# Two decoder layers on one Trainium2 core: the last MLP's second tile in banks of 512, 256 and 256 columns, and a mean square that ACT adds at the layer boundaries

## The chip, the cores and the metric

The kernel runs on one core of a Trainium2 chip. The metric is the device time of one execution in microseconds (us). Five engines work side by side, each through its own queue in order: PE (TensorE, matrix products; "PEld" is its weight load), DVE (VectorE), ACT (ScalarE), POOL (GpSimd) and SP (SyncE, which here issues DMAs). An engine waits for another by a semaphore; what stands behind a waiting instruction in its queue waits too.

## The reference, cut to what matters

Two layers run over 256 tokens of 1024 features. Each layer has a mixer (block-sparse and indexed attention) and a gated MLP of width 2816, both in the same sandwich:

```
h = rms_norm(x, g_pre) * (1 + scale) + shift
y = token_mixer(h)            # or: (gelu(conv3(h @ w_up_act)) * (h @ w_up_lin)) @ w_down
x = x + gate * rms_norm(y, g_post)

rms_norm(v, g) = v * rsqrt(mean(v * v) + 1e-6) * g      # mean over the 1024 features, per token
```

So each of the four sub-layers ends with the mean square of `y` per token, and three of them go on with the mean square of the new `x`, before the next product can start. The last sub-layer ends with the output's DMA.

## The kernel before, in words

The 256 tokens are two tiles of 128 rows (t = 0 and 1). Weights come through a stream of 1 MB DMAs into `raw` and are split there into a high and a low fp32r part: ACT copies the high one (`wh`, `dh`, line 139), DVE subtracts it for the low one (`wl`, `dl`, line 140). Every product is then three passes on PE (`mm3`, lines 567 to 569, or `project`, line 391): high x high, low x high, high x low.

The MLP goes through 22 blocks of 128 hidden features. `up(i)` makes a block's hidden activations, 24 matmuls of 256 columns for each of the two branches, and `down` multiplies them by `w_down`: for each tile t two PSUM banks of 512 output columns, `ys[t]`, three matmuls for each bank and block. The banks collect all 22 blocks. 17 of the blocks go through `down` between the `up`s; the last five follow at the end, first tile 0's two banks, then tile 1's.

`residual` ends a sub-layer for one tile. For each bank it takes the squares' sum over 512 columns on ACT (`square`, line 254, an activation and a read of its accumulator) and multiplies by the gate on DVE (line 318). `inv_root` then lets POOL add the two sums and EPS (line 262) and raise that to -0.5 (line 264), and DVE adds the result to `xt` (line 326). At the very end the pieces are sent to DRAM from there, tile 1 in pieces of 512, 256 and 256 columns.

`boundary` joins two sub-layers. There are three: mixer to MLP in layer 0 (near 153 to 175 us in the trace), MLP to the next layer's mixer (near 342 to 366 us), and mixer to MLP in layer 1 (near 483 to 506 us). In each, `stat` takes the mean square of the new `xt` in two halves on ACT and `inv_root` again finishes it on POOL; `norm_T` scales by it on DVE (line 286) and PE turns the result (line 274); `mod_T` makes `hh` and `hl` from it, on ACT (lines 297, 307, 305) and DVE (lines 300, 309). PE's next products need these.

The order on each engine is not the order of the code. A scheduler places the instructions by its own estimates, except where the code pins them or says that one is issued after another; so an added or lengthened instruction can move others.

Of the kernel before, what the change touches and what calls it, by code (L numbers as in the profile page):

```python
# [12 lines left out]
BF = mybir.dt.bfloat16  # L13
AF = mybir.ActivationFunctionType
OP = mybir.AluOpType
AX = mybir.AxisListType

D = 1024
S = 256
DEPTH = 2  # L20
HD = 64
FF = 2816
NF = FF // 128
EPS = 1e-6
# [50 lines left out]
def trunk(ctx: ExitStack, tc, plan, x, c, stream, small, rope, out):  # L75
    nc = tc.nc
# [10 lines left out]
    def bank(i):  # L87
        return ps.tile([128, 512], F32, name=f"b{i}", tag=f"b{i}")
# [7 lines left out]
    def t2(dt=F32):  # L96
        return wrk.tile([128, 512], dt, name="t2", tag="t2", bufs=12)
# [4 lines left out]
    def tiny(n):  # L102
        return wrk.tile([128, n], F32, name=f"tiny{n}", tag=f"tiny{n}", bufs=8)
# [113 lines left out]
    def pre_scale(l, which):  # L217
        a = wrk.tile([128, 8], F32, name="prescale", tag="prescale", bufs=2)
        o = 8 if which == "mix" else 32
        nc.vector.scalar_tensor_tensor(out=a, in0=mods[l][:, o:o + 8], scalar=1.0,  # L220
                                       in1=scol(l, "g_pre_" + which)[:, :8], op0=OP.add, op1=OP.mult)
        return a, mods[l][:, o - 8:o]
# [29 lines left out]
    def square(src, n, s, to=None):  # L252

        nc.scalar.activation(out=t2(BF) if to is None else to, in_=src, func=AF.Square, scale=float(n) ** -0.5, accum_out=s)  # L254

    def inv_root(s):

        r = tiny(1)
        if s.shape[-1] == 1:
            nc.gpsimd.tensor_scalar(out=r, in0=s, scalar1=EPS, scalar2=None, op0=OP.add)  # L260
        else:
            nc.gpsimd.tensor_scalar(out=r, in0=s[:, 0:1], scalar1=s[:, 1:2], scalar2=EPS, op0=OP.add, op1=OP.add)
        r2 = tiny(1)
        nc.gpsimd.tensor_tensor(out=r2, in0=r, in1=mhalf, op=OP.pow)
        return r2
# [11 lines left out]
    def stat(t):  # L277
        s = tiny(2)
        for h in range(2):
            square(xt[:, t, 512 * h:512 * h + 512], D, s[:, h:h + 1])  # L280
        return inv_root(s)

    def norm_T(t, r, banks):
        xn = [t2(), t2()]
# [26 lines left out]

    def residual(t, y, g, to=None):

        s = tiny(2)
        d = [t2(), t2()]
        for h in range(2):
            square(y[h], D, s[:, h:h + 1])
            nc.vector.tensor_tensor(out=d[h], in0=y[h], in1=g[:, 512 * h:512 * h + 512], op=OP.mult)
            if h == 0:
                yield  # L320
        r = inv_root(s)
        yield
        parts = [(0, 512), (512, 256), (768, 256)] if to is not None and t else [(0, 512), (512, 512)]
        for i, (o, n) in enumerate(parts):
            xo = xt[:, t, o:o + n]
            nc.vector.scalar_tensor_tensor(out=xo, in0=d[o // 512][:, o % 512:o % 512 + n], scalar=r, in1=xo,
                                           op0=OP.mult, op1=OP.add)
            if to is not None:
                (nc.scalar if i % 2 else nc.sync).dma_start(to[:, o:o + n], xo)
        yield  # L330

    def boundary(ys, g, scale, bias, hh, hl):

        r0, r1 = residual(0, ys[0], g), residual(1, ys[1], g)
        for _ in range(3):
            next(r0)
        s0 = stat(0)
        next(r1)
        p0 = norm_T(0, s0, (4, 5))
        next(r1)  # L340

        def second(ins):
            with tc.issue_after(ins):
                next(r1)

        a = mod_T(p0, 0, scale, bias, hh, hl, second)
        s1 = stat(1)
        p1 = norm_T(1, s1, (6, 4))
        return a, mod_T(p1, 1, scale, bias, hh, hl)
# [216 lines left out]
    def mm3(y, hh, hl, wh, wl, first, last):  # L566
        nc.tensor.matmul(y, lhsT=hh, rhs=wh, start=first, stop=False)  # L567
        nc.tensor.matmul(y, lhsT=hl, rhs=wh, start=False, stop=False)  # L568
        nc.tensor.matmul(y, lhsT=hh, rhs=wl, start=False, stop=last)  # L569
# [10 lines left out]
    def half(a, h):  # L580
        return a[:, 512 * h:512 * h + 512]
# [181 lines left out]
    for l in range(DEPTH):  # L763
# [90 lines left out]
        ys = [[bank(0), bank(1)], [bank(2), bank(3)]]  # L854
# [40 lines left out]
        scale, bias = pre_scale(l, "ffn")  # L895
# [5 lines left out]
        ys = [[bank(0), bank(1)], [bank(2), bank(3)]]  # L901
# [22 lines left out]
        def up(i):  # L924
# [27 lines left out]
            nc.vector.tensor_tensor(out=al, in0=av, in1=ah.bitcast(F32), op=OP.subtract)  # L952
            pend.append((i, ah, al, dh, dl))

        def down(items, tiles):
            for t in tiles:
                tt = slice(128 * t, 128 * t + 128)
                for h in range(2):
                    for i, ah, al, dh, dl in items:
                        mm3(ys[t][h], ah[:, tt], al[:, tt], half(dh, h), half(dl, h), i == 0, i == NF - 1)  # L960
                        yield

        for i in range(NF):
            if i == 3 + 4 * l:
                bg.add("ada", gemv_v(l, 40, 48, 4))
                bg.add("ada", gate_rows(l, "ffn"))
                if l + 1 < DEPTH:
                    bg.add("ada", gemv_v(l + 1, 0, 32, 5))
            bg.run(up(i))
            if i < NF - 3 and len(pend) > 2:  # L970
                bg.run(down([pend.pop(0)], (0, 1)))
        bg.drain("ada")
        gate = gates["ffn"]
        bg.run(down(pend, (0, 1)))
        tps["free"] = [6, 7]
        if l + 1 < DEPTH:
            hh, hl = hT_tiles()
            scale, bias = pre_scale(l + 1, "mix")

            placed = boundary(ys, gate, scale, bias, hh, hl)  # L980
        else:
            for t in range(2):
                for _ in residual(t, ys[t], gate, out[0, 128 * t:128 * t + 128, :]):
                    pass
# [79 lines left out]
```

## Time and profile before

| | us |
|---|---|
| median of 3 runs (lowest, highest) | 689.65 (689.32, 689.72) |
| the profiled execution | 690.58 |
| its span, first to last instruction | 688.8 |
| busy in the span: PE, DVE, ACT, POOL | 665.0, 549.9, 424.8, 26.2 |

PE is busy for 97% of the span at a mean granted clock of 0.995 of full speed, so the time is PE's work plus the few places where it waits, plus the tail behind its last matmul. The profiled execution's own time is 1.8 us above its span and 0.9 us above the median. Columns of the views used here: start, duration, engine, line, operation, what it writes and reads, shapes, count; in brackets the idle time before and what ended it. A matmul's duration is its whole passage through the array; what a stream of them costs is the distance between starts. Lines are those of the kernel before.

### The profile page before, as it was taken

Reading aid. Unit: us, or ns where it says so; the run is one execution under the profiler, and the core shown is the slowest. Engines: PE = TensorE matmul, PEld = TensorE weight load, DVE = VectorE, ACT = ScalarE, POOL = GpSimd, SP = SyncE. Lnnn points to the kernel's source line nnn. Section 1 sums busy time; section 2 is a strip of 40 time slices with the busy share of each in tenths; the row PEclk is TensorE's granted clock in tenths of the full one; section 3 lists DMA queues with packets and bytes.
Section 4 is the critical chain, followed back from the end, with each engine's and each line's share of the span. In section 5 each row is a group of like instructions: output and inputs, shape, how many; then the busy total and the mean of one; then the engine's idle time right before and its main releaser. Section 6 shows DMA issues by size and latency. Waiting matters only on the chain.

```text
span 688.8 us, 11284 instructions
## 1 busy us (share of the span) xinstructions
PE 665.0 (97%) x4311; PEld 570.4 (83%) x4311; DVE 549.9 (80%) x1088; ACT 424.8 (62%) x786; POOL 26.2 (4%) x56
## 2 busy tenths in 40 slices
PE   7999898999999999999999999999999999999996
PEld 4787676777999999999988677777789999999994
DVE  5898999978899999897679985677689876666553
ACT  5566677886955555455576558868696555555441
POOL 1000000002000000000020000000200000000001
PEclk9999999999999999999999999999999999999999
DMA  9999548963489999987436732346246885644001
GB/s 363 419 415 378 181 169 331 368 248 122 184 319 376 380 365 340 341 326 282 163 151 240 279 131 116 123 166 218 107 164 236 303 332 179 224 184 183 1 1 62
DMA packets 24519, 163.04 MB, mean 237 GB/s; under 512 B 3313, under 2 KB 3729, under 8 KB 6161
## 3 DMA queue, kind: packets, MB, share of 16 engines
q1 hardware_dynamic: 23184, 159.77, 61.6%
q0 software_dynamic: 704, 2.11, 1.1%
q8 instruction: 34, 0.56, 0.3%
q10 hardware_dynamic: 576, 0.43, 0.2%
q14 instruction: 21, 0.16, 0.1%
HBM read 161.24 MB, written 1.06 MB: 236 GB/s over the span
## 4 chain that ended last, share of the span: by engine, by line
PE 76%; DVE 12%; ACT 6%; issue 3%; POOL 1%; DMA 1%; SPq 0%; POOLq 0%; DVEq 0%; ACTq 0%
PE b L569 18%; PE b L567 18%; PE b L568 18%; PE b L391 13%; DVE wl L140 3%; PE b L411 3%; DVE raw L684 2%; DVE iscore L434 2%; ACT t L479 1%; PE b L494 1%; ACT t L254 1%; DMA raw<-in_stream_dram 1%; PE b L726 1%; DVE iscore L446 1%; PE b L274 1%
## 5 line engine op out<-in xcount | busy, mean ns | idle before, releaser
L140 DVE TENSOR_TENSOR wl<-raw,wh 128x1024 fp32r<-128x1024 f32 (+1 forms) x146 | 173.1, 1197 | 36.8 <-ACT wh L139 31.2
L567 PE MATMUL b<-hh,wh 128*128 128x256 f32 x640 | 180.1, 281 | 0.0
L569 PE MATMUL b<-hl,wh 128*128 128x256 f32 x640 | 179.7, 281 | 0.0
L568 PE MATMUL b<-hh,wl 128*128 128x256 f32 x640 | 179.7, 281 | 0.0
L139 ACT ACTIVATE wh<-raw 128x1024 fp32r<-128x1024 f32 (+1 forms) x146 | 148.9, 1046 | 43.9 <-PE b L569 36.2
L568 PEld LDWEIGHTS b<-hh,wl 128*128 128x128 f32 x640 | 122.5, 191 | 1.3
L567 PEld LDWEIGHTS b<-hh,wh 128*128 128x128 f32 x640 | 120.2, 188 | 1.5
L569 PEld LDWEIGHTS b<-hl,wh 128*128 128x128 f32 x640 | 120.2, 188 | 0.0
L189 DVE SCALAR_TENSOR_TENSOR raw<-raw,crow 128x1024 f32<-128x1024 f32 x72 | 86.7, 1220 | 1.3 <-DMA raw<-in_stream_dram 1.3
L391 PE MATMUL b<-wh,hh 128*128 128x512 f32 (+1 forms) x184 | 73.0, 400 | 0.1
L391 PE MATMUL b<-wh,hl 128*128 128x512 f32 (+1 forms) x184 | 68.8, 389 | 0.0
L140 DVE TENSOR_TENSOR dl<-raw,dh 128x1024 fp32r<-128x1024 f32 (+2 forms) x47 | 56.9, 1213 | 13.7 <-ACT dh L139 12.9
L139 ACT ACTIVATE dh<-raw 128x1024 fp32r<-128x1024 f32 (+2 forms) x47 | 49.5, 1058 | 25.9 <-PE b L568 25.9
L944 ACT ACTIVATE t<-b,smt 128x256 f32<-128x256 f32 x44 | 25.0, 569 | 57.9 <-PE b L569 57.9
L567 PE MATMUL b<-dh,t 128*128 128x512 f32 x152 | 59.7, 393 | 0.0
L568 PE MATMUL b<-dh,t 128*128 128x512 f32 x152 | 59.6, 392 | 0.0
L569 PE MATMUL b<-dl,t 128*128 128x512 f32 x152 | 59.2, 389 | 0.0
L391 PE MATMUL b<-wl,hh 128*128 128x512 f32 (+1 forms) x184 | 56.6, 398 | 0.9 <-DVE wl L140 0.9
L391 PEld LDWEIGHTS b<-wh,hh 128*128 128x128 f32 x184 | 34.7, 188 | 8.7 <-issue 1.7
L391 PEld LDWEIGHTS b<-wl,hh 128*128 128x128 f32 x184 | 34.5, 193 | 7.2 <-DVE wl L140 1.2
L391 PEld LDWEIGHTS b<-wh,hl 128*128 128x128 f32 x184 | 34.0, 189 | 6.2 <-issue 0.6
L945 DVE SCALAR_TENSOR_TENSOR t<-b,smt,t 128x255 f32<-128x255 f32 x44 | 21.2, 482 | 20.6 <-ACT t L944 20.4
(172 smaller groups left out, 1100.0 us busy)
## 6 DMA issues: line engine op xcount, KB each, us to landing
raw<-in_stream_dram SPq DMA_DIRECT2D x143, 1024.0 KB, 6.3
raw<-in_stream_dram SPq DMA_DIRECT2D x8, 804.0 KB, 9.9
gate<-gated POOLq DMA_DIRECT2D x4, 512.0 KB, 8.5
xt<-in_x_dram SPq DMA_DIRECT2D x2, 512.0 KB, 4.2
raw<-in_stream_dram SPq DMA_DIRECT2D x1, 984.0 KB, 4.9
out_dram<-xt SPq DMA_DIRECT2D x2, 256.0 KB, 2.1
raw<-in_stream_dram SPq DMA_DIRECT2D x1, 328.0 KB, 5.1
out_dram<-xt ACTq DMA_DIRECT2D x1, 256.0 KB, 2.1
```

The costliest lines, as they stand in the source:

```text
L139: put(nc.scalar.activation(out=hi[:, :n], in_=raw, func=AF.Copy))
L140: put(nc.vector.tensor_tensor(out=lo[:, :n], in0=raw, in1=hi[:, :n].bitcast(F32), op=OP.subtract))
L189: nc.vector.scalar_tensor_tensor(out=ri, in0=ri, scalar=1.0, in1=crow, op0=OP.mult, op1=OP.mult, accum_out=mods[l][:, j + i:j + i + 1])
L391: mm = lambda l_, k, i, start=False, stop=False: nc.tensor.matmul(a[:, :n], lhsT=l_[:, k, tt], rhs=w[k][i], start=start, stop=stop)
L411: ins = nc.tensor.matmul(out, lhsT=lhsT, rhs=rhs, **flags)
L434: nc.vector.scalar_tensor_tensor(out=sc, in0=r[:, j * nk:j * nk + nk], scalar=wi[:, h:h + 1], in1=fill[:, 256 - nk:] if first else sc, op0 ...
L567: nc.tensor.matmul(y, lhsT=hh, rhs=wh, start=first, stop=False)
L568: nc.tensor.matmul(y, lhsT=hl, rhs=wh, start=False, stop=False)
L569: nc.tensor.matmul(y, lhsT=hh, rhs=wl, start=False, stop=last)
L684: pin(nc.vector.scalar_tensor_tensor(out=r, in0=r, scalar=1.0, in1=crow, op0=OP.mult, op1=OP.mult, accum_out=mods[0][:, 8 * a + k:8 * a + ...
L944: nc.scalar.activation(out=z, in_=p[:, :256], func=AF.Identity, scale=w2[:, i:i + 1], bias=bc[:, i:i + 1])
L945: nc.vector.scalar_tensor_tensor(out=z[:, 1:], in0=p[:, :255], scalar=w1[:, i:i + 1], in1=z[:, 1:], op0=OP.mult, op1=OP.add)
```

## The change

Three edits. In the last layer's MLP tile 1's output lies in three banks, one of 512 columns and two of 256 (a part of bank 3, and of bank 7), and `down` runs over these; each 512-column matmul of the former second bank is two of 256. `residual` for this tile takes three sums of squares; POOL adds the first two and EPS, and DVE adds the third when it is there. And in `stat`, at all three boundaries, POOL adds EPS to the first half's sum, and an ACT activation (Identity with a bias) adds the second half's; POOL then has the power alone.

```diff
-    def inv_root(s):
+    def inv_root(s, last=None):
         r = tiny(1)
-        if s.shape[-1] == 1:
-            nc.gpsimd.tensor_scalar(out=r, in0=s, scalar1=EPS, scalar2=None, op0=OP.add)
+        if last is nc.scalar:
+            nc.scalar.activation(out=r, in_=s[:, 1:2], func=AF.Identity, bias=s[:, 0:1])
+        elif last is nc.vector:
+            nc.vector.tensor_tensor(out=r, in0=s[:, 0:1], in1=s[:, 1:2], op=OP.add)
         else:
             nc.gpsimd.tensor_scalar(out=r, in0=s[:, 0:1], scalar1=s[:, 1:2], scalar2=EPS, op0=OP.add, op1=OP.add)
...
             square(xt[:, t, 512 * h:512 * h + 512], D, s[:, h:h + 1])
-        return inv_root(s)
+            if h == 0:
+                nc.gpsimd.tensor_scalar(out=s[:, :1], in0=s[:, :1], scalar1=EPS, scalar2=None, op0=OP.add)
+        return inv_root(s, nc.scalar)
...
+            s, early = tiny(4), tiny(2)
+            for i, (o, n) in enumerate([(0, 512), (512, 256), (768, 256)]):
+                square(y[i], D, early[:, 1:2] if i == 2 else s[:, i:i + 1], t2(BF)[:, :n])
+                if i == 1:
+                    nc.gpsimd.tensor_scalar(out=early[:, :1], in0=s[:, 0:1], scalar1=s[:, 1:2], scalar2=EPS,
+                                            op0=OP.add, op1=OP.add)
+                if i == 2:
+                    r = inv_root(early, nc.vector)
+                nc.vector.tensor_tensor(out=d[o // 512][:, o % 512:o % 512 + n], in0=y[i], in1=g[:, o:o + n],
+                                        op=OP.mult)
...
+        if l == DEPTH - 1:
+            ys[1] = [bank(2), bank(3)[:, :256], bank(7)[:, :256]]
...
-                for h in range(2):
+                o = 0
+                for y in ys[t]:
+                    n = y.shape[-1]
                     for i, ah, al, dh, dl in items:
-                        mm3(ys[t][h], ah[:, tt], al[:, tt], half(dh, h), half(dl, h), i == 0, i == NF - 1)
+                        mm3(y, ah[:, tt], al[:, tt], dh[:, o:o + n], dl[:, o:o + n], i == 0, i == NF - 1)
                         yield
+                    o += n
```

The scheduler also places other work differently with it. The lines of the changed kernel are some 3 to 20 higher for the same instruction (254 stays, 274 is 277, 286 is 291, 297 is 302, 300 is 305, 305 is 310, 307 is 312, 309 is 314, 326 is 345, 391 is 410); line 261 is the new addition on ACT. Numbers behind a name count tiles and differ between the two.

ACT at the boundary from layer 0's MLP to layer 1's mixer, tile 1 (`tiny2` the two sums, `wh` splits of weights that later products need), before:

```order
L254 ACTIVATE t2_3872,tiny2_3869<-xt_69 128x512
L139 ACTIVATE wh_4087<-raw_4085 128x1024
L139 ACTIVATE wh_4091<-raw_4085 128x1024
L297 ACTIVATE hh_3795<-b6_3882,mod1_100,prescale_3797 128x128 x4
L307 ACTIVATE t2_3892<-b6_3882,mod1_100,prescale_3797 128x128 x2
L305 ACTIVATE hh_3795<-t2_3893 128x4x128
L307 ACTIVATE t2_3892<-b6_3882,mod1_100,prescale_3797 128x128 x2
```

and with the change:

```order
L254 ACTIVATE t2_3876,tiny2_3872<-xt_69 128x512
L139 ACTIVATE wh_4091<-raw_4089 128x1024
L261 ACTIVATE tiny1_3878<-tiny2_3872 128x1
L139 ACTIVATE wh_4095<-raw_4089 128x1024
L139 ACTIVATE wh_4101<-raw_4099 128x1024
L302 ACTIVATE hh_3797<-b6_3886,mod1_100,prescale_3799 128x128 x4
L312 ACTIVATE t2_3896<-b6_3886,mod1_100,prescale_3799 128x128 x4
L310 ACTIVATE hh_3797<-t2_3897 128x4x128
```

The addition stands behind a weight split, a third split has come in front of tile 1's `hh`, and `hh`'s second half (line 305, now 310) stands behind four activations of line 307 (now 312) where it stood behind two.

PE at the same place: line 274 (now 277) turns tile 1, `b2` is tile 0's first product in layer 1, `b1` its second, `b0` tile 1's first. Before:

```order
L391 MATMUL b2_3929<-dh_3925,hl_3796 128x328
L274 MATMUL b6_3882<-ident_75,t2_3878 128x128 x4
L274 MATMUL b4_3887<-ident_75,t2_3879 128x128 x4
L391 MATMUL b2_3929<-dh_3925,hl_3796 128x328
L391 MATMUL b1_4015<-wl_4012,hh_3795 128x256
L391 MATMUL b1_4015<-wh_4011,hh_3795 128x256
L391 MATMUL b1_4015<-wl_4012,hh_3795 128x256
L391 MATMUL b0_3967<-dh_3915,hh_3795 128x328
L391 MATMUL b0_3967<-dl_3916,hh_3795 128x328
L391 MATMUL b1_4015<-wh_4011,hh_3795 128x256
```

and with the change:

```order
L410 MATMUL b2_3933<-dh_3929,hl_3798 128x328 x2
L410 MATMUL b1_4019<-wl_4016,hh_3797 128x256
L410 MATMUL b1_4019<-wh_4015,hh_3797 128x256
L410 MATMUL b1_4019<-wl_4016,hh_3797 128x256
L410 MATMUL b1_4019<-wh_4015,hh_3797 128x256
L410 MATMUL b1_4019<-wl_4016,hh_3797 128x256
L410 MATMUL b1_4019<-wh_4015,hh_3797 128x256
L410 MATMUL b1_4019<-wl_4016,hh_3797 128x256
L410 MATMUL b1_4019<-wh_4011,hl_3798 128x256 x4
L410 MATMUL b1_4019<-wh_4015,hl_3798 128x256 x3
L277 MATMUL b6_3886<-ident_75,t2_3882 128x128 x4
L277 MATMUL b4_3891<-ident_75,t2_3883 128x128 x4
```

One matmul of 328 columns and 14 of 256 have come in front of the turn of tile 1, seven more of which (`wl`/`wh` with `hh`, and `hl`) formerly lay between those of `b0`; behind the turn there is now one matmul of `b1`, and then only `b0`: eight on the first half of `hh`, eight on the second, eight on `hl`.

DVE at the third boundary (mixer to MLP, layer 1), tile 0: line 286 (now 291) makes the two halves that PE turns, line 140 is a weight split. Before:

```order
L326 SCALAR_TENSOR_TENSOR xt_69<-t2_5302,tiny1_5311,xt_69 128x512
L318 TENSOR_TENSOR t2_5325<-b2_5035,gate_4127 128x512
L286 TENSOR_SCALAR t2_5330<-xt_69,tiny1_5322 128x512
L140 TENSOR_TENSOR wl_5231<-raw_5224,wh_5230 128x1024
L286 TENSOR_SCALAR t2_5331<-xt_69,tiny1_5322 128x512
```

and with the change:

```order
L345 SCALAR_TENSOR_TENSOR xt_69<-t2_5305,tiny1_5315,xt_69 128x512
L324 TENSOR_TENSOR t2_5329<-b2_5039,gate_4131 128x512
L140 TENSOR_TENSOR wl_5235<-raw_5228,wh_5234 128x1024
L291 TENSOR_SCALAR t2_5335<-xt_69,tiny1_5327 128x512
L291 TENSOR_SCALAR t2_5336<-xt_69,tiny1_5327 128x512
```

Both halves now stand behind the weight split. On ACT the addition for this tile stands behind the split's other half, `wh_5234`. PE's order is the same there as before.

## Rows read from the trace of the kernel before

**Rows 1.** Timeline of PE, last MLP: start, duration, line, operation, shapes, count.
```profile
651.08 0.28 PE L567 MATMUL b<-hh,wh 128*128 128x256 f32 x1
...
668.04 0.40 PE L567 MATMUL b<-dh,t 128*128 128x512 f32 x1
...
678.58 0.40 PE L567 MATMUL b<-dh,t 128*128 128x512 f32 x1
...
681.81 0.40 PE L569 MATMUL b<-wl,t 128*128 128x512 f32 x1
```

**Rows 2.** Timeline of all engines, the tail behind the last matmul.
```profile
682.80 0.19 ACT L254 ACTIVATION_READ_ACCUMULATOR t<-b 128x1 f32 x1
...
683.09 0.30 POOL L262 TENSOR_SCALAR tiny<-tiny 128x1 f32<-128x1 f32 x1 [6.03 <-ACT t L254]
683.47 0.56 POOL L264 TENSOR_TENSOR tiny<-tiny,mhalf 128x1 f32<-128x1 f32 x1
684.07 1.54 DVE L326 SCALAR_TENSOR_TENSOR xt<-t,tiny,xt 128x512 f32<-128x512 f32 x3 [0.35 <-POOL tiny L264]
```

**Rows 3.** ACT by line and form: count, then busy us, mean ns of one.
```profile
L517 ACT ACTIVATE t<-b 128x256 f32<-128x256 f32 x8 | 3.0, 376 | 1.5 <-PE b L411 1.4
...
L517 ACT ACTIVATE t<-b 128x512 f32<-128x512 f32 x4 | 2.3, 582 | 0.0
...
L595 ACT ACTIVATE tiny<-mhalf 128x1 f32<-128x1 f32 x2 | 0.4, 202 | 0.0
```

**Rows 4.** DVE by line and form, one value per row.
```profile
L551 DVE TENSOR_SCALAR tiny<-b 128x1 f32<-128x1 f32 x8 | 1.3, 157 | 4.0 <-PE b L549 4.0
```

**Rows 5.** Timeline of all engines, second boundary (MLP to mixer), tile 1.
```profile
357.54 2.04 ACT L139 ACTIVATE wh<-raw 128x1024 fp32r<-128x1024 f32 x2
357.59 1.21 PE L391 MATMUL b<-dh,hl 128*128 128x328 f32 x7
...
358.77 0.88 DVE L286 TENSOR_SCALAR t<-xt,tiny 128x512 f32<-128x512 f32 x2 [0.94 <-POOL tiny L264]
359.31 1.12 PE L274 MATMUL b<-ident,t 128*128 128x128 f32 x8 [0.51 <-DVE t L286]
...
360.00 1.50 ACT L297 ACTIVATE hh<-b,mod,prescale 128x128 fp32r<-128x128 f32 x4 [0.42 <-PE b L274]
...
361.39 0.82 ACT L307 ACTIVATE t<-b,mod,prescale 128x128 f32<-128x128 f32 x2
...
364.59 1.36 PE L391 MATMUL b<-dh,hl 128*128 128x328 f32 x8
...
365.79 0.28 PE L391 MATMUL b<-wh,hh 128*128 128x256 f32 x1
```

**Rows 6.** Timeline of all engines, third boundary (mixer to MLP, layer 1).
```profile
490.73 1.05 ACT L139 ACTIVATE wh<-raw 128x1024 fp32r<-128x1024 f32 x1
...
491.47 0.48 DVE L286 TENSOR_SCALAR t<-xt,tiny 128x512 f32<-128x512 f32 x1
...
493.77 1.50 ACT L297 ACTIVATE hh<-b,mod,prescale 128x128 fp32r<-128x128 f32 x4
...
496.17 0.66 ACT L305 ACTIVATE hh<-t 128x512 fp32r<-128x512 f32 x1
...
496.89 0.50 PE L391 MATMUL b<-dh,hh 128*128 128x512 f32 x1 [0.50 <-ACT hh L305]
...
500.02 0.55 PE L274 MATMUL b<-ident,t 128*128 128x128 f32 x3 [0.33 <-DVE t L286]
```

**Rows 7.** Timeline of PE, first boundary, turn of tile 1.
```profile
170.29 1.12 PE L274 MATMUL b<-ident,t 128*128 128x128 f32 x8 [0.29 <-DVE t L286]
```

**Rows 8.** Waits of PE over the span: us in total, times, longest.
```profile
PE b L368 <- ACT wh L139: 1.2, 1, 1.2
PE b L368 <- DVE t L362: 1.1, 2, 0.7
```

**Rows 9.** Timeline of DVE, shortly before the first of those waits.
```profile
380.43 2.36 DVE L140 TENSOR_TENSOR wl<-raw,wh 128x1024 fp32r<-128x1024 f32 x2 [0.59 <-PE b L391]
```

More of the change, by code (lines that the diff above doesn't have):

```diff
@@ L312, in residual @@
     def residual(t, y, g, to=None):
-        s = tiny(2)
         d = [t2(), t2()]
-        for h in range(2):
[L317 to L321, printed above, removed]
+        if len(y) == 2:
+            s = tiny(2)
+            for h in range(2):
+                square(y[h], D, s[:, h:h + 1])
+                nc.vector.tensor_tensor(out=d[h], in0=y[h], in1=g[:, 512 * h:512 * h + 512], op=OP.mult)
+                if h == 0:
+                    yield
+            r = inv_root(s)
+        else:
+            s, early = tiny(4), tiny(2)
[8 more added lines that the diff above has]
+                                        op=OP.mult)
+            yield
         yield
@@ L957, in down @@
                 tt = slice(128 * t, 128 * t + 128)
-                for h in range(2):
+                o = 0
+                for y in ys[t]:
+                    n = y.shape[-1]
                     for i, ah, al, dh, dl in items:
-                        mm3(ys[t][h], ah[:, tt], al[:, tt], half(dh, h), half(dl, h), i == 0, i == NF - 1)
+                        mm3(y, ah[:, tt], al[:, tt], dh[:, o:o + n], dl[:, o:o + n], i == 0, i == NF - 1)
                         yield
+                    o += n
         for i in range(NF):
```

## The prediction

> **What bounds the kernel now.** I read the page's busy times first: PE 665.0 us of a span of 688.8, so a term counts only if it lengthens PE's stream, opens or closes a wait of PE, or lies behind its last matmul. Then I read the timelines at the four places that the change touches. In [rows 1] the reader is to see the pitch of the last MLP's stream, from start to start; in [rows 2] the serial chain behind the last square, from ACT's accumulator read over two POOL operations to DVE. [Rows 5 to 7] show the three boundaries, each with a wait of PE for the turned tile, and in [rows 5] how long ACT needs behind the turn before it is done with `hh`. Last I read the waits and what precedes one of them [rows 8, 9], to see whether a shift would be absorbed later.
>
> The sum is made against the profiled execution (span 688.8, own time 690.58, 0.9 above the median) and its difference is put on the median of 689.65. A measurement here can tell about 0.2% from no change, 1.38 us; so "slower" begins at 691.03 and "faster" at 688.27.
>
> **Last MLP, the banks.** 66 matmuls of 512 columns (22 blocks, 3 passes) become 132 of 256. 144 matmuls of 256 lie between 651.08 and 668.04: 16.96/144 = 0.1178 us each. 14 of 512 lie between 678.58 and 681.81: 3.23/14 = 0.2307 [rows 1]. Two of 256 cost 0.2356, so each replaced matmul costs 0.0049 more, and 66 cost **+0.32**. All lie on the stream of a busy PE, so nothing hides them. These 256-column matmuls have a weight load each, as the new ones will, so the pitch is bounded well: zero below, about 0.6 above if the halves cost twice that surplus.
>
> The Trainium skill ("TensorE: Matmul & The Clock Gate", section "Back-to-back issue gap") gives an isolated gap of 262 cycles for 256 columns and 518 for 512; a pair would cost 6 cycles more, 2.5 ns at 2.4 GHz, as an estimate from that page 0.17 us for the 66, and the whole sum would come out at 1.31 us. The trace has 4.9 ns [rows 1], nearly twice that, and the trace decides.
>
> **Last MLP, the tail.** The last square covers 256 columns instead of 512: 376 ns instead of 582 [rows 3], -0.21. Behind its accumulator read (682.80 + 0.19 = 682.99), POOL's addition starts 0.10 later, takes 0.30, and 0.08 later, at 683.47, the power starts: 0.48 [rows 2]. The new chain is ACT to DVE (I take 0.10, as ACT to POOL), one addition of one value (0.157, the nearest DVE row [rows 4]), and DVE to POOL (I take 0.04, the step from the power's end at 684.03 to DVE at 684.07 [rows 2]): 0.30, so -0.18. Handoffs of 0.04 both or 0.10 both give -0.24 and -0.12. Together **-0.39**, and with the banks the last MLP gives -0.07 (0 to -0.13). The third product with the gate on DVE is as long as half of the former one and runs beside the square; it costs nothing.
>
> **The three boundaries, ACT's addition.** By itself the edit replaces POOL's addition between accumulator and power (0.48, as above) by an ACT activation on one value: 0.08 (an engine waiting for its own last result, as POOL does between its two steps), 0.20 ([rows 3], line 595, the nearest form) and 0.10 to POOL, 0.38: -0.10 where it is bound to nothing else. It is an ACT instruction, though, and stands in ACT's queue; what precedes it there is now part of PE's chain.
>
> First boundary. Tile 1's addition follows its accumulator read directly, and PE is idle for 0.29 before the turn [rows 7], so the 0.10 comes through: **-0.10** (0 if the self-wait is 0.18).
>
> The Trainium skill ("ScalarE: Activation LUTs", section "Rules for kernel authors") budgets about 0.3 us for an ACTIVATE whose bias is a pointer operand. The row nearest to ours has 0.20 [rows 3]; no row of before has this form. By the page the gain at this boundary and at tile 1 of the third would be zero, and the sum 0.2 higher.
>
> Second boundary, tile 1 [rows 5]. ACT's addition stands behind one split more than the squares (the order of ACT in the part on the change). Two splits take 2.04 from 357.54, so the first ends at 358.56; then 0.20, 0.10 to POOL and 0.56 for the power: 359.42. DVE has the low split of 1.18 (2.36 for two [rows 9]) in front of both halves of the norm, to 359.8. Before, the norm started at 358.77 and PE turned 0.54 later; now 359.8 + 0.54 = 360.35.
>
> PE has been given work for that time: one 328-column matmul (0.15: eight lie between 364.59 and 365.79) and 14 of 256 (0.1178) stand in front of the turn, 1.80 in all. Before, the seven matmuls from 357.59 ended at 358.64; now PE reaches the turn at 358.64 + 1.80 = 360.44, later than 360.35. So the idle 0.51 in front of the turn goes, and the turn starts at 360.44 instead of 359.31.
>
> What is late next is `hh`. Line 297 starts 0.69 behind the turn (359.31 to 360.00), and four activations take 1.39 (to 361.39), 0.35 each; now eight of them stand in front of the copy that makes `hh`'s second half: 2.78. That copy reaches PE 0.72 after its start (496.17 to 496.89 [rows 6], the same form). So PE can take that half at 360.44 + 0.69 + 2.78 + 0.72 = 364.63. Behind the turn (1.12) PE has only one matmul of `b1` and eight of `b0` on the first half left, some 1.4 us, that are ready no earlier than 0.69 + 1.39 + 0.72 behind it; the 14 that would have filled the gap have been spent in front. PE waits some 1.6 to 2.0 us in this stretch, ended by ACT. Then 16 matmuls of 0.15 and 0.10 for the first behind a wait (0.50 against 0.40 [rows 6, 1]) bring the end to 364.63 + 2.50 = 367.13. Before, this work ended at 365.79. **+1.34**. The lower bound is a PE without waits behind the turn: from 360.44, the 6.48 between 359.31 and 365.79 less the 1.80 already done, 365.12, **-0.67**. The upper is +2.0, if each of the eight activations costs 0.08 more for standing before a copy. I take the computed value, since each piece of it has its row.
>
> Third boundary, tile 0 [rows 6]. ACT's split runs from 490.73 to 491.78, the addition stands behind it, and DVE's low split now precedes both halves of the norm instead of lying between them (the order of DVE). The first half could start at 491.47 before; now the split comes first, the halves end near 493.43 and PE turns; line 297 starts 0.69 to 0.70 behind the turn, 494.16 instead of 493.77: 0.39 later. That passes to PE's wait at 496.89, and the squares that follow. Tile 1's addition gives 0.10 back before the turn at 500.02, where PE waits 0.33: **+0.29** (0 to +0.5).
>
> **Sum.** -0.07 - 0.10 + 1.34 + 0.29 = +1.46: span 690.3, profiled execution 692.0, median **691.1**.
>
> **Rivals.** (a) *PE does not wait behind the second turn.* ACT is early there, because the scheduler's estimate is right and the activations of line 312 overlap with PE's `b0`. Then the term is -0.67, and the sum -0.55: 689.1. For it: 1.80 us of PE's work was moved to where PE was idle for 0.51 [rows 5]. Against it: `hh`'s copy behind eight activations of 0.35, and PE's own rows behind the turn.
>
> (b) *The lateness is given back.* Later PE waits three times, 2.3 us in all, for splits that ACT and DVE make of weights [rows 8]; splits done earlier at the boundary could shorten these, and the end is then 1.46 - 2.3 = -0.84: 688.8, and if a little more is gained, faster beyond the bound. This is the case on the other side: it decides if DVE and ACT reach those splits by their own clock. Against it: DVE itself waits 0.59 for PE shortly before [rows 9], so that the later waits move with PE.
>
> (c) *The detour costs more.* ACT's one-value activation behind its own accumulator read waits longer than 0.08, and the halves of 512 columns are bound by their weight loads: 0.2 more at each of two places, 0.3 for the banks, 0.3 at the second boundary. The sum is 1.46 + 1.0 = 2.46: 692.1.
>
> (d) *Nothing that can be measured*, in that the boundary takes only half: +0.67 instead of 1.34, sum 0.79, 690.4. It is the low part of the forecast's own case.
>
> **How the numbers follow.** The forecast's case (a wait of PE behind the second turn, sum +0.8 to +2.0) gets 0.66, of which 0.42 lies above 1.38 and 0.24 below it, as the sum stands just above the bound; its own range is 690.4 to 691.7. (c) gets 0.08, all slower. (a) gets 0.17: 0.15 within the bound and 0.02 faster; (b) 0.09: 0.05 within and 0.04 faster. So faster 0.06, same 0.44, slower 0.50. The range reaches down into (a) and up into (c): it leaves out (b), 0.09, some 0.06 of (a) and half of (c), 0.04, so 689.0 to 692.0.
>
> **What the profile after would show.** Right: at the second boundary PE's wait in front of the turn is gone and the turn starts some 1.1 us later; behind it PE waits 1.6 us or more, ended by ACT's line 310; the boundary's last matmul starts 1.3 later. At the third, the turn of tile 1 starts 0.3 later than the second boundary's shift alone gives. The waits of [rows 8] are as long as before. The former 512-column bank's matmuls have a pitch of 0.118, and from the last matmul to DVE's last additions 0.39 is gone. Wrong: no wait of PE ended by line 310 (then (a)), or waits of [rows 8] shortened by about the shift (then (b)), or a pitch above 0.125 or an addition above 0.3 us (then (c)).

## The result: 3.4 us slower, where 1.5 was forecast

| | before | with the change |
|---|---|---|
| median, us (lowest, highest) | 689.65 (689.32, 689.72), 689.81 with three later runs | 693.03 (692.90, 693.83) |
| ratio to before, 95% interval | | 1.0051 (1.0041, 1.0061) |
| span of the profiled execution | 688.8 | 691.2 |
| busy: PE, DVE, ACT, POOL | 665.0, 549.9, 424.8, 26.2 | 664.6, 550.7, 426.5, 31.2 |

The kernel is slower, as forecast, but by more than twice as much, and 693.03 lies above the range of 689.0 to 692.0. PE has as much work as before; POOL is busy for 5 us longer, with as many operations as before (56).

The spans of the two profiled executions differ by 2.4 us, less than the medians, because the one of before lost 1.24 us ahead of anything that the change touches. The same turn of a tile in layer 0's mixer starts at 131.62 before and at 130.38 after; before's first 100 us had a mean granted clock of 0.98, after's 1.00. So I measure from that turn. First the row of before, then those of after: the timeline of PE at the markers, with the columns as ahead of the prediction.

```profile
131.62 0.63 PE L494 MATMUL b<-ident,t 128*128 128x128 f32 x4 [0.51 <-DVE t L487]
...
384.61 0.63 PE L368 MATMUL b<-ident,t 128*128 128x128 f32 x4 [0.46 <-DVE t L362]
```

```profile
130.38 0.63 PE L513 MATMUL b<-ident,t 128*128 128x128 f32 x4 [0.51 <-DVE t L506]
...
169.20 1.00 PE L277 MATMUL b<-ident,t 128*128 128x128 f32 x7 [0.46 <-DVE t L291]
...
385.26 0.63 PE L387 MATMUL b<-ident,t 128*128 128x128 f32 x4 [0.47 <-DVE t L381]
...
501.77 1.11 PE L277 MATMUL b<-ident,t 128*128 128x128 f32 x8 [0.45 <-DVE t L291]
...
684.66 0.28 PE L588 MATMUL b<-wl,t 128*128 128x256 f32 x1
```

The distances from that turn, and what each stretch adds to before (the first boundary ends at tile 1's turn, 170.29 [rows 7]; the second at the turn at 384.61; the third at tile 1's turn, 500.02 [rows 6]; the stream at the last matmul's start and one pitch, 681.81 + 0.23 before and 684.66 + 0.12 after [rows 1]; the tail at the last power's start, 683.47 [rows 2] and 685.86):

| stretch, us | before, to its end | after | added | forecast |
|---|---|---|---|---|
| first boundary | 38.67 | 38.82 | +0.15 | -0.10 |
| second boundary | 252.99 | 254.88 | +1.74 | +1.34 |
| third boundary | 368.40 | 371.39 | +1.10 | +0.29 |
| PE's stream in the last MLP | 550.42 | 554.40 | +0.99 | +0.32 |
| tail | 551.85 | 555.48 | -0.35 | -0.39 |
| sum | | | +3.63 | +1.46 |

Now the second boundary, all engines, after (answering to [rows 5]):

```profile
356.20 0.89 POOL L285 TENSOR_SCALAR tiny<-tiny 128x1 f32<-128x1 f32 x1 [2.79 <-ACT t L254]
...
356.63 1.05 ACT L139 ACTIVATE wh<-raw 128x1024 fp32r<-128x1024 f32 x1
357.58 0.28 ACT L261 ACTIVATE tiny<-tiny 128x1 f32<-128x1 f32 x1
357.71 1.23 DVE L140 TENSOR_TENSOR wl<-raw,wh 128x1024 fp32r<-128x1024 f32 x1 [0.70 <-ACT wh L139]
...
357.94 1.42 POOL L267 TENSOR_TENSOR tiny<-tiny,mhalf 128x1 f32<-128x1 f32 x1 [0.85 <-ACT tiny L261]
359.40 0.88 DVE L291 TENSOR_SCALAR t<-xt,tiny 128x512 f32<-128x512 f32 x2 [0.46 <-POOL tiny L267]
...
359.94 1.11 PE L277 MATMUL b<-ident,t 128*128 128x128 f32 x8 [0.30 <-DVE t L291]
...
364.11 0.42 PE L410 MATMUL b<-dh,hh 128*128 128x328 f32 x1 [1.35 <-ACT hh L310]
```

The reader is to see the queue first: ACT's addition (L261) stands behind a split. Then POOL's power (L267): DVE's low split (L140) has begun 0.23 us earlier, and the power, 0.56 in [rows 2], takes 1.42 and ends 0.42 behind the split. DVE's norm waits for the power (0.46), not for the split. Last, PE waits 1.35 behind the turn, ended by `hh`'s second half. The power of before at this place, where DVE ran nothing:

```profile
358.17 0.56 POOL L264 TENSOR_TENSOR tiny<-tiny,mhalf 128x1 f32<-128x1 f32 x1
```

The third boundary, tile 0 (answering to [rows 6]), has the same picture:

```profile
491.38 1.05 ACT L139 ACTIVATE wh<-raw 128x1024 fp32r<-128x1024 f32 x1
...
492.33 0.28 ACT L261 ACTIVATE tiny<-tiny 128x1 f32<-128x1 f32 x1
492.46 1.22 DVE L140 TENSOR_TENSOR wl<-raw,wh 128x1024 fp32r<-128x1024 f32 x1 [0.26 <-ACT wh L139]
...
492.69 1.42 POOL L267 TENSOR_TENSOR tiny<-tiny,mhalf 128x1 f32<-128x1 f32 x1 [2.14 <-ACT tiny L261]
...
494.14 0.88 DVE L291 TENSOR_SCALAR t<-xt,tiny 128x512 f32<-128x512 f32 x2 [0.46 <-POOL tiny L267]
...
494.63 0.56 POOL L265 TENSOR_SCALAR tiny<-tiny 128x1 f32<-128x1 f32 x1 [0.52 <-ACT t L254]
```

The last row is `residual`'s addition for tile 1: it runs beside the norm, which has one large SBUF input, and takes 0.56 where [rows 2] have 0.30.

And the first, tile 1, where no queue stands in the way (answering to [rows 7]): POOL's early addition of EPS runs beside DVE's two `hl` (L314, from 166.27 and 166.88) and takes 0.71, so ACT's addition waits 0.22 for it, behind its own accumulator read:

```profile
166.94 0.71 POOL L285 TENSOR_SCALAR tiny<-tiny 128x1 f32<-128x1 f32 x1 [3.49 <-ACT t L254]
167.23 0.23 ACT L254 ACTIVATION_READ_ACCUMULATOR t<-xt 128x1 f32 x1
167.68 0.30 ACT L261 ACTIVATE tiny<-tiny 128x1 f32<-128x1 f32 x1 [0.22 <-POOL tiny L285]
168.06 0.57 POOL L267 TENSOR_TENSOR tiny<-tiny,mhalf 128x1 f32<-128x1 f32 x1 [0.41 <-ACT tiny L261]
```

From accumulator (167.46) to power it is 0.60 instead of 0.48. Tile 0's power there takes 1.42 too (at 160.07, beside a low split), but the turn of tile 0 comes no later than before, 31.74 behind the marker instead of 31.72.

The tail does nearly what was forecast (answering to [rows 2]): 0.35 from accumulator (685.51) to power, where 0.30 was said.

```profile
685.32 0.19 ACT L254 ACTIVATION_READ_ACCUMULATOR t<-b 128x1 f32 x1
685.61 0.16 DVE L263 TENSOR_TENSOR tiny<-tiny 128x1 f32<-128x1 f32 x1 [1.43 <-ACT t L254]
...
685.86 0.56 POOL L267 TENSOR_TENSOR tiny<-tiny,mhalf 128x1 f32<-128x1 f32 x1 [1.73 <-DVE tiny L263]
```

### The profile page after: what moved, and what is told of

It reads as the page before. It is cut to its first block, busy times and chain, and to the rows that moved or that the text cites. A ratio compares the mean times of both kernels' runs of the same rounds, so it can differ in the third digit from the quotient of the medians.

```text
span 691.2 us, 11425 instructions
## 1 busy us (share of the span) xinstructions
PE 664.6 (96%) x4377; PEld 571.7 (83%) x4377; DVE 550.7 (80%) x1090; ACT 426.5 (62%) x794; POOL 31.2 (5%) x56
## 3 DMA queue, kind: packets, MB, share of 16 engines
q1 hardware_dynamic: 23184, 159.77, 61.4%
## 4 chain that ended last, share of the span: by engine, by line
PE 73%; DVE 14%; ACT 7%; issue 3%; POOL 2%; DMA 1%; SPq 0%; POOLq 0%; DVEq 0%; ACTq 0%
PE b L588 18%; PE b L587 18%; PE b L586 18%; PE b L410 12%; DVE wl L140 3%; PE b L430 2%; DVE raw L703 2%; DVE iscore L453 2%; ACT t L498 1%; DVE iscore L465 1%; ACT t L254 1%; DVE tiny L464 1%; PE b L513 1%; DMA raw<-in_stream_dram 1%; PE b L745 1%
## 5 line engine op out<-in xcount | busy, mean ns | idle before, releaser
L140 DVE TENSOR_TENSOR wl<-raw,wh 128x1024 fp32r<-128x1024 f32 (+1 forms) x146 | 173.2, 1198 | 37.7 <-ACT wh L139 30.9
L140 DVE TENSOR_TENSOR dl<-raw,dh 128x1024 fp32r<-128x1024 f32 (+2 forms) x47 | 56.9, 1213 | 14.5 <-ACT dh L139 13.7
L587 PE MATMUL b<-dh,t 128*128 128x512 f32 (+1 forms) x171 | 63.1, 369 | 0.0
L586 PE MATMUL b<-dh,t 128*128 128x512 f32 (+1 forms) x171 | 63.0, 369 | 0.0
L588 PE MATMUL b<-dl,t 128*128 128x512 f32 (+1 forms) x171 | 62.5, 366 | 0.0
```

The source lines that it names most:

```text
L140: put(nc.vector.tensor_tensor(out=lo[:, :n], in0=raw, in1=hi[:, :n].bitcast(F32), op=OP.subtract))
```

## The experiments

Theory A: the boundaries make most of the loss, by the places of ACT's addition in its queue and by POOL waiting for DVE. Against it B (the banks), C (the new addition itself is slow wherever it stands) and D (POOL is late for another reason). Each kernel's stretches, measured as above, in us against before; the time is its median against the runs of before that were made with it (for the change against 689.65; against all six runs of before it is +3.2).

| kernel | first | second | third | stream | tail | sum | time |
|---|---|---|---|---|---|---|---|
| the change | +0.15 | +1.74 | +1.10 | +0.99 | -0.35 | +3.63 | +3.4 |
| e1_banks | 0.01 | 0.02 | 0 | +1.03 | -0.36 | +0.70 | +0.58 |
| e2_stat | +0.14 | +1.70 | +1.14 | +0.05 | 0 | +3.03 | +3.01 |
| e5_b2_free | +0.13 | +0.30 | +1.12 | +0.94 | -0.35 | +2.14 | +2.14 |
| e12_b2_low_late | +0.13 | +0.74 | +1.11 | +1.01 | -0.35 | +2.64 | +2.63 |
| e10_b2_b3_free | -0.37 | +0.49 | +0.16 | +0.99 | -0.35 | +0.92 | +0.76 |
| e9_no_early | -0.03 | +1.86 | +0.95 | +0.97 | -0.36 | +3.40 | +3.72 |
| e6_dve_add | 0.01 | -0.12 | +0.03 | +0.19 | 0 | +0.11 | -0.09 |
| e7_last_item | 0.02 | -0.22 | +0.05 | +0.07 | +0.61 | +0.53 | +0.40 |
| e11_dve_all | +1.14 | +0.63 | +0.12 | +2.04 | +0.40 | +4.33 | +4.36 |

The stretches add up to the times to within 0.4 us. Each row of stretches is one execution; how far that can be trusted shows in e8_pool_probe below, the kernel before with work off the path, whose stretches are those of before to within 0.04.

**One half of the change at a time: e1_banks and e2_stat.** e1_banks keeps `stat` as before; e2_stat drops this from the changed kernel (and its `residual` then has two banks again):

```diff
-        if l == DEPTH - 1:
-            ys[1] = [bank(2), bank(3)[:, :256], bank(7)[:, :256]]
```

> The kernel before with the three banks of the last MLP alone; the boundaries keep POOL's addition, and every engine's order there is that of before. Theory A (the boundaries make most of the loss): 0.4 to 0.6 us slower than before; PE's stream from the third boundary to its last matmul 0.8 to 1.0 longer, the tail from the last matmul to the power 0.45 shorter; no wait of PE at the second boundary's second half above 0.3. Theory B (the banks make most of it): 2 us slower or more. The forecast's term was -0.07.

> The kernel before with ACT's addition at the three boundaries alone; the last MLP keeps two banks of 512 columns. Theory A: 2.7 to 3.1 us slower than before, in three places: 0.1 to 0.2 at the first boundary, 1.7 at the second, 1.0 to 1.1 at the third; POOL's power beside a weight split on DVE takes 1.42 us instead of 0.56. Theory B: 1 us slower or less. The forecast's sum for it was 1.53.

690.08, a ratio of 1.0006 (0.9997 to 1.0015), and 692.51, 1.0037 (1.0023 to 1.0051). Their losses add up to the whole, and each lies in its own stretches. B falls: the boundaries make 3.0 of 3.4 to 3.6. The banks alone are not a gain either: the stream's +1.0 takes more than the tail gives, though e1's time alone cannot be told from before.

**Queue and power at the second boundary: e5_b2_free and e12_b2_low_late.** Both start from the changed kernel. In e5 the later weight splits are issued behind ACT's addition (`st["added"]` is that instruction); in e12 only DVE's low split is put behind the norm (`st["normed"]`).

```diff
-            st["behind"] = placed[0]
+            st["behind"] = (*placed[0], st["added"])     # e5: ACT's addition of tile 1
+            st["behind"] = (*placed[0], st["normed"])    # e12: DVE's last norm of tile 1
```

> The changed kernel, but at the second boundary the weight splits stand behind ACT's addition; PE's turn stands again in front of the 14 matmuls of 256 columns there. Theory A (the place in the queues costs, not the addition): the second boundary's 1.72 us falls to 0.3 or less, so about 1.5 us faster than the changed kernel, 1.9 slower than before; the power there takes 0.56 again, since no split on DVE runs beside it; PE's wait of 1.35 ended by ACT's hh is gone. Rival C (the addition itself is slow on ACT, with its early step on POOL): within 0.4 us of the changed kernel.

> The changed kernel; at the second boundary only DVE's low split is put behind the two halves of the norm, while ACT's addition stays behind ACT's split as in the change. It separates ACT's queue from POOL's wait for DVE. If POOL's wait is a part of its own: POOL's power takes 0.57 there instead of 1.42, the turn of tile 1 comes 0.7 to 0.9 us earlier, and with it the split of PE's work around the turn goes back in part, so 1.0 to 1.5 us faster than the changed kernel. If the place in ACT's queue is all: the power still ends at the same time and the turn comes within 0.2 us of the changed kernel's.

691.64, 1.0026 (1.0016 to 1.0035), and 692.23, 1.0037 (1.0023 to 1.0051). e12's five times lie from 691.29 to 693.33 and its interval overlaps the change's, so what it says rests on its stretches and rows. All engines in e12, second boundary:

```profile
357.00 1.04 ACT L139 ACTIVATE wh<-raw 128x1024 fp32r<-128x1024 f32 x1
357.94 0.28 ACT L261 ACTIVATE tiny<-tiny 128x1 f32<-128x1 f32 x1
...
358.31 0.57 POOL L267 TENSOR_TENSOR tiny<-tiny,mhalf 128x1 f32<-128x1 f32 x1 [0.85 <-ACT tiny L261]
...
359.45 0.79 PE L277 MATMUL b<-ident,t 128*128 128x128 f32 x5 [0.27 <-DVE t L291]
...
362.93 0.42 PE L410 MATMUL b<-dh,hh 128*128 128x328 f32 x1 [0.21 <-ACT hh L310]
```

ACT's addition is as late as in the changed kernel, but the power has its 0.57 again. The turn comes 0.72 earlier (measured from the turn at 131.62 and its like), and the scheduler leaves seven of the 14 matmuls behind it, so that PE's wait of 1.35 shrinks to 0.21. The boundary goes from +1.74 to +0.74. Freeing ACT's queue as well (e5) takes it to +0.30. So of 1.74 us, taken off in this order, 1.0 hung on DVE's split beside the power, with what the scheduler had moved for it, and 0.44 on ACT's queue. Both parts of A hold. The 0.30 that is left is, by its rows, the same wait of POOL once more. All engines in e5, second boundary:

```profile
357.25 0.30 ACT L261 ACTIVATE tiny<-tiny 128x1 f32<-128x1 f32 x1 [0.40 <-POOL tiny L285]
```

POOL's early addition takes 0.89 beside DVE's two `hl`, as in the row at 356.20 of the change, where tile 0's at the third boundary takes 0.22 (490.33) with DVE idle. From the accumulator (356.84) to the power (357.62) it is 0.78, and 0.48 before. In the change itself the split in ACT's queue hides this. Less the 0.40 that ACT waits for POOL, the chain is 0.38 and no longer than before; so by these rows, though no run takes that wait away alone, little is left of C.

**The third boundary: e10_b2_b3_free.** As e5, and the split that stood in front of tile 0's addition is traced behind it:

```diff
...
         s0 = stat(0)
+        if mid:
+            with tc.issue_after(st["added"]):
+                mid()                  # the loose split of the next weights
...
```

> As e5_b2_free, and at the two boundaries from mixer to MLP the loose weight split stands behind ACT's addition of tile 0 as well. Theory A: the third boundary's turn of tile 0 comes 0.7 to 1.0 us earlier, POOL's power there takes 0.57 instead of 1.42, and the kernel is 0.7 to 1.0 us faster than e5_b2_free, 690.8, which leaves the banks' 0.5 and some 0.5 for ACT's addition. Rival C: no change against e5_b2_free.

690.25, 1.0014 (1.0005 to 1.0023). The third boundary's +1.1 falls to +0.16, and the first even gains, 0.50 against e5: tile 0's power there has 0.57 too (at 159.77), and its turn comes 0.6 earlier than in the change. It was 1.4 us faster than e5, more than expected, because I had not counted the first boundary. The second boundary, edited as in e5, is at +0.49 instead of +0.30; I did not look into that. All engines, third boundary, tile 0:

```profile
489.69 0.28 ACT L261 ACTIVATE tiny<-tiny 128x1 f32<-128x1 f32 x1
...
489.88 1.05 ACT L139 ACTIVATE wh<-raw 128x1024 fp32r<-128x1024 f32 x1
490.06 0.57 POOL L267 TENSOR_TENSOR tiny<-tiny,mhalf 128x1 f32<-128x1 f32 x1 [1.19 <-ACT tiny L261]
```

**What POOL waits for: e8_pool_probe.** Off the path, in blocks 8 to 17 of layer 0's MLP:

```diff
                 hi, lo = split(raws.pop(0))
+                if l == 0 and 8 <= i < 18:
+                    nc.gpsimd.tensor_tensor(out=tiny(1), in0=hi[:, :1].bitcast(F32), in1=mhalf, op=OP.pow)
+                    nc.gpsimd.tensor_scalar(out=tiny(2)[:, :1], in0=hi[:, :1].bitcast(F32), scalar1=EPS, scalar2=None, op0=OP.add)
+                    for _ in range(6):
+                        nc.gpsimd.memset(tiny(2), 0.0)
```

> The kernel before with, in ten blocks of layer 0's MLP, probes on POOL behind ACT's weight split, off the path: one power and one addition of a value per partition, which read SBUF, and six memsets, which only write. No result of them is used. Theory A (POOL waits while DVE runs an operation with two SBUF inputs): the power, which becomes ready together with DVE's low split, takes 1.3 to 1.5 us where the split starts first, the addition 0.3 or up to 1.2, and the memsets about 0.1 throughout. Rival D (POOL's operations are long for another reason, such as ACT's or the DMA's traffic, or a late semaphore): memsets are stretched as well, or the powers keep 0.56.

POOL by line and form, the probes (L933, L934, L936) and the kernel's own powers (L264); count, busy us, mean ns:

```profile
L933 POOL TENSOR_TENSOR tiny<-wh,mhalf 128x1 f32<-128x1 f32 x20 | 27.3, 1365 | 69.7 <-ACT wh L139 69.7
L934 POOL TENSOR_SCALAR tiny<-wh 128x1 f32<-128x1 f32 x20 | 14.2, 709 | 1.7
L264 POOL TENSOR_TENSOR tiny<-tiny,mhalf 128x1 f32<-128x1 f32 x14 | 7.8, 561 | 1.2
...
L936 POOL MEMSET tiny<- 128x2 f32 x120 | 5.1, 99 | 1.1
```

A piece of the timelines of POOL and of DVE:

```profile
250.21 1.55 POOL L933 TENSOR_TENSOR tiny<-wh,mhalf 128x1 f32<-128x1 f32 x1
251.84 0.22 POOL L934 TENSOR_SCALAR tiny<-wh 128x1 f32<-128x1 f32 x1
...
252.36 1.60 POOL L933 TENSOR_TENSOR tiny<-wh,mhalf 128x1 f32<-128x1 f32 x1
```

```profile
250.12 1.21 DVE L140 TENSOR_TENSOR wl<-raw,wh 128x1024 fp32r<-128x1024 f32 x1
...
251.88 0.48 DVE L952 SCALAR_TENSOR_TENSOR t<-b,smt,t 128x254 f32<-128x254 f32 x1
252.31 1.22 DVE L140 TENSOR_TENSOR wl<-raw,wh 128x1024 fp32r<-128x1024 f32 x1
```

The one run took 689.74. 19 of the 20 powers began 0.03 to 0.90 us behind the start of a DVE operation with two SBUF inputs, a low split or line 189's product (`raw<-raw,crow`), and each of them ended 0.40 to 0.43 behind that operation's end, after 0.75 to 1.61; the twentieth ran beside operations on PSUM (`b`) and took 0.57. Of the additions 16 took 0.70 to 1.13 and ended 0.08 behind such an operation; the four others, like the one between the two powers shown, took 0.22. DVE's low splits and line 189's products keep their 1.2 throughout. The 120 memsets, which read nothing, kept 0.1 us. So D falls. The Trainium skill says this ("SBUF — State Buffer", section "Who interferes with whom"): a DVE instruction with two SBUF inputs contends with a GpSimd instruction that reads SBUF, not with one that only writes it. The probes agree, with 1365 ns against 561 and 99. The same section of the Trainium skill says that issue order decides who blocks. The probes show POOL blocked when DVE came first; where POOL came first (e6's first boundary, a low split 0.26 behind the start of a power) both kept their length, 0.57 and 1.22.

**Is the early addition to blame: e9_no_early.** POOL's early addition of EPS is taken out of `stat`, and EPS is left out of the boundaries' mean square; the order of all else is that of the changed kernel.

> The changed kernel without POOL's early addition of EPS to the first half's mean square at the boundaries; EPS is left out there, the order of everything else is that of the changed kernel. Theory A: the early addition is on the path only at tile 1 of the first and third boundary, where it is stretched to 0.70 and ACT waits 0.22 for it: 0.3 to 0.5 us faster than the changed kernel, and nothing at the second boundary. Rival C (the early step is what costs most): 1.5 us faster or more.

693.21, 1.0051 (1.0039 to 1.0064). The stretches show -0.17 at the first and -0.15 at the third boundary against the change, and +0.12 at the second; the time does not show it. I had expected 0.3 to 0.5 us; the gain in the two stretches is 0.3, the second boundary takes some of it back, and in the time none is seen. The early step is not what makes the loss: C, as far as it blames that step, falls.

**Another engine for the addition: e6_dve_add, e11_dve_all.** e6 is the kernel before with `inv_root(s, nc.vector)` in `stat`, EPS added early by POOL as in the change; e11 does the same in `residual` too.

> The kernel before, with the second half's mean square added by DVE instead of POOL or ACT (EPS early by POOL as in the change); two banks of 512. DVE's queue holds the addition in front of the weight splits. Theory A: accumulator to power in 0.35 to 0.40 instead of 0.48, and nothing else moves much: 0.1 to 0.4 us faster than before. Rival C (taking the addition from POOL costs by itself, whichever engine gets it, because POOL's early step or the handoffs are slow): 0.3 us slower than before or more.

> As e6_dve_add (two banks of 512, DVE adds the second half at the boundaries), and residual's mean square is added by DVE as well, with EPS put in early by POOL. From the traces: accumulator to power 0.35 instead of 0.48 at the end of the kernel and in front of the boundaries' new x, so 0.1 to 0.4 us faster than before, 689.2. Rival: the scheduler's other order, or POOL's early step beside DVE's long operations, takes that back: no faster than before.

e6: 689.41, 0.9998 (0.9989 to 1.0007), no difference, where 0.1 to 0.4 us was expected. DVE's addition is in front of the low splits, the power has 0.57 at all six places, and the time gained there is too small to be seen. e11: 693.96, 1.0063 (1.0050 to 1.0076), my expectation of 689.2 missed by 4.8 us. At the first boundary DVE goes from its addition straight on to the next long operation, so the power ran into that:

```profile
156.63 0.15 DVE L263 TENSOR_TENSOR tiny<-tiny 128x1 f32<-128x1 f32 x1
156.70 1.22 DVE L189 SCALAR_TENSOR_TENSOR raw<-raw,crow 128x1024 f32<-128x1024 f32 x1
```

```profile
156.87 1.48 POOL L267 TENSOR_TENSOR tiny<-tiny,mhalf 128x1 f32<-128x1 f32 x1 [4.12 <-DVE tiny L263]
```

That is the same price at a place that the change had not touched; its other +2.0 is in the last MLP, where PE waits 1.59 us near 517 us for DVE's line 967. In DVE's queue a low split now stands between line 965 and that one (515.22), where the same two followed each other before (512.70, 513.21): another order. I did not follow it up further.

**Only the last block in halves: e7_last_item.** e6, with 512 columns for all blocks but the last, whose two halves lie in one bank.

```diff
...
+                    for q in range(2):
+                        mm3(y[:, 256 * q:256 * q + 256], ah[:, tt], al[:, tt], dh[:, 512 + 256 * q:768 + 256 * q],
+                            dl[:, 512 + 256 * q:768 + 256 * q], False, q == 1)
...
+            ys[1] = [ys[1][0], ys[1][1][:, :256], ys[1][1][:, 256:]]
```

> DVE's addition at the boundaries (as in e6_dve_add), and of tile 1's second bank in the last MLP only the last block's three matmuls are two halves of 256 columns in one bank; the sums for it are taken in three pieces as in the change. If the pitch of the 132 short matmuls is what ate the tail's gain: 0.35 to 0.45 us faster than e6_dve_add, 689.0, and PE's blocks in the last MLP are 8.40 us apart again. If the banks' cost comes from something else in the change (the three sums, the order of the splits): no faster than e6_dve_add.

689.89, 1.0004 (0.9995 to 1.0013): no gain on e6, where 0.35 to 0.45 was expected. The stream's cost is gone, so the 132 short matmuls and what goes with them do make it. But the tail is 0.61 longer instead of 0.35 shorter. ACT's rows in the tail:

```profile
680.99 0.39 ACT L254 ACTIVATE t<-b 128x256 bf16<-128x256 f32 x1 [2.68 <-PE b L588]
...
681.96 0.39 ACT L254 ACTIVATE t<-b 128x256 bf16<-128x256 f32 x1 [0.49 <-DVE t L338]
```

The first square starts only when the bank's last matmul is done (680.62 + 0.28 and the handoff), and the second waits for DVE's product of the first half. With one bank, ACT, DVE and PE take turns at it in this program (whether the chip or the program's own dependences order them was not tested); the change, with a bank for each half, does not have this wait. Of all versions none beats the kernel before by more than its interval.

## Why the prediction was wrong

- **The failed step** is "0.56 for the power: 359.42", at the second boundary, and its unspoken copy at the third. The 0.56 came from rows in which DVE ran nothing with two SBUF inputs beside it. I had moved DVE's low split in front of the norm in the next sentence, and so beside the power. It took 1.42. The turn was 1.72 late, not 1.13 (359.94 + 1.09 - 359.31, 1.09 being what the changed kernel's profiled execution was ahead by at the first boundary's turn). Of the 2.17 us between the forecast and the stretches' sum, this step makes 0.40 at the second boundary and 0.57 at the third; the stream of the last MLP makes 0.67, tile 1's addition 0.25 at the first boundary and 0.24 at the third. The clue was in the trace of before, in a row that I had grouped away: the power of line 553 beside a low split of DVE.

```profile
115.58 1.45 POOL L553 TENSOR_TENSOR tiny<-tiny,mhalf 128x1 f32<-128x1 f32 x1 [19.65 <-DVE tiny L551]
```

```profile
115.42 1.22 DVE L140 TENSOR_TENSOR wl<-raw,wh 128x1024 fp32r<-128x1024 f32 x1
```

- **What held at the second boundary**: the idle 0.51 in front of the turn nearly went (0.30), the next lateness was `hh`'s second half, and PE waited for it: 1.35 where 1.6 to 2.0 was said. Rival (a) is out. The later waits of [rows 8] kept their length (2.3 in all, by the page's waits of PE: "L387 <- DVE t L381", 3 times), so rival (b) is out too.
- **Third boundary, +0.29 forecast, +1.10 measured.** I let the norm start behind the low split (492.95) and the power end earlier. The power ended 0.43 behind the split instead, and the norm behind that: tile 0's `hh` (line 297, now 302) started 0.96 later, not 0.39 (495.38 - 0.65 - 493.77, 0.65 being what the changed execution was ahead by at the second boundary's end). Tile 1's addition, which was to give 0.10 back, cost the other 0.14, by the same two sizes as at the first boundary. With ACT's place and the split moved, 0.16 was left (e10).
- **First boundary, -0.10 forecast, +0.15 measured.** Two sizes: ACT's activation on one value took 0.28 to 0.30 us, not the 0.20 of [rows 3], and POOL's early addition, which I had off the path, ended 0.19 behind the accumulator. On the first the Trainium skill ("ScalarE: Activation LUTs", section "Rules for kernel authors") was right with about 0.3 for a pointer bias, and I had gone by the row of another form.
- **The stream, +0.32 forecast, +0.99 measured.** In steady blocks the gelu's start, one per block, moves on by 58.80 us in seven blocks before and by 59.03 after, 8.400 and 8.433 each:

```profile
598.14 0.56 ACT L944 ACTIVATE t<-b,smt 128x256 f32<-128x256 f32 x1 [1.77 <-PE b L569]
...
656.94 0.56 ACT L944 ACTIVATE t<-b,smt 128x256 f32<-128x256 f32 x1 [1.77 <-PE b L569]
```

```profile
600.55 0.56 ACT L963 ACTIVATE t<-b,smt 128x256 f32<-128x256 f32 x1 [1.77 <-PE b L588]
...
659.58 0.57 ACT L963 ACTIVATE t<-b,smt 128x256 f32<-128x256 f32 x1 [1.77 <-PE b L588]
```

  That is 0.011 for each of three pairs, twice the 0.0049 that I took from the unmixed streams of [rows 1]. The short matmuls keep their pitch, six of them 0.71 us (593.98 to 594.69 after); it is the long ones that were cheaper among short ones, three of them 0.68 us (591.60 to 592.28 before), 0.226 each and not 0.2307. 17 blocks make 0.56, the last five some 0.07. Another 0.14 are two gaps at the first block's `down` (after, starts at 524.17, 524.44 and 524.77, so 0.27 and 0.33 instead of 0.23); e1, whose stream is as long, does not have them there, so they go with this kernel's order. The last 0.2 lies in one block. Before, 39 matmuls of 256 columns behind a small one for the gates (line 232) run at 0.113 each (576.72 to 581.14); with the change that small one stands inside `down`, and the 256-column ones behind it run at 0.118 (48 from 577.83 to 583.48). Why the pitch was shorter there is open; the granted clock is 1.00 in both.

- **The tail**, -0.39 forecast, -0.35 measured. Right.
- **The rivals.** (c), at 692.1, came nearest. Its 0.2 more at each of two places was nearly right (0.25 and 0.24), as was its 0.3 at the second boundary (0.40), but for another reason: ACT waited for POOL's early addition, not for itself. It had 0.3 for the banks (0.67), and it too had nothing for the power beside the split at the third boundary. Its signs, a pitch above 0.125 or an addition above 0.3, did not show. (d) is out, as the second boundary took more than the computed value.

## What to carry to other kernels

A short operation's duration is that of its surroundings: before a row's mean is moved to a new place, look at its longest instance and at what the neighbour engine ran then. A step that is taken from one engine's queue to another's costs what stands in front of it there, and the scheduler moves other work with it; here a saving of 0.1 us at the second boundary cost 1.0 beside DVE's split and 0.4 in ACT's queue. Splitting a product for an earlier tail is paid on every pass of the stream, and the tail gets it back once.

## What the runs showed of the hardware that was not expected

- POOL's power on one value per partition takes 0.75 to 1.61 us instead of 0.56, and an addition 0.70 to 1.13 instead of 0.22, when DVE's 1.2 us operation with two SBUF inputs has begun first: in the profile a longer instruction, not idle time. The power ends 0.40 to 0.43 behind DVE's operation, the addition 0.08. A memset keeps its 0.1 (e8). DVE's operation is not lengthened (1.21 to 1.23 beside the probes). A norm of DVE with one large SBUF input stretched an addition too, 0.56 instead of 0.30 (the change, 494.63).
- A pair of 256-column matmuls in a mixed stream costs 0.011 us more than one of 512 columns, which takes 0.226 there; in runs of one kind it is 0.005, with 0.231 for the long one.
